# Orders of their own for the last four attention rounds, the last three query tiles' exponentials transposed by TensorE

## The chip, the cores and the metric

The kernel runs on one core of a Trainium2 chip. The metric is the device time of one execution in microseconds. Of the kernel before three executions were timed; their median is the time it is known by. One more execution was taken with the hardware profiler, and all rows in this document come from that one. TensorE is the matmul engine (PE in the rows), VectorE is DVE, ScalarE is ACT, GpSimd is POOL, and SP issues the DMAs.

## What is computed

One transformer-like layer over 1024 latent tokens of width 1024 and 256 context tokens. Its parts: layer norm and modulation, one input projection, latent attention with 8 heads, a Fourier mixing branch, gates, one output projection, and a residual with a last layer norm. What matters here, cut from the reference:

```python
s = einsum("bqhd,bkhd->bhqk", q, k) / sqrt(96)        # 1280 keys: 256 context, 1024 latent
p = softmax(s, axis=-1)
attn = einsum("bhqk,bkhv->bqhv", p, v)
y = concatenate([attn * silu(g_mla), four * silu(g_f)], -1) @ w_out + b_out
x_new = layer_norm(2 ** 0.25 * x + gate * y, post_ln_g, post_ln_b)
```

## The kernel before

Products that need f32 accuracy are done as three matmuls on a high and a low part (`mm3`); softmax weights and V are split into two f16 parts.

Attention works in 32 rounds, one for each pair of query tiles of one head: `Pair` n has head n // 4 and the query tiles j = 0 and 1, each 128 queries by 1280 keys. The steps for a tile:

- S: the scores, on TensorE, into PSUM. `SL[j]` holds 1024 latent keys, and `SC`, which both tiles share, the context keys.
- m, c, t: minima over both parts, with a copy into the SBUF tile `E`, and the bias, on VectorE.
- x: the exponential of 1280 columns in place, on ScalarE.
- h, l: the f16 high part on ScalarE and the low part by subtraction on GpSimd, into a tile `EH`, and then one transposing DMA from `EH` to half of `ET` (line 1058). There are three buffers each of `E`, `EH` and `ET`.
- P0, P1: PV over five key blocks each, on TensorE, for both tiles of a pair at a time, into a PSUM tile of the pool `tr`, which has three buffers.
- Ra, Rv: the two parts of PV are added into `ats` by ScalarE and VectorE.

The loop at the end of the attention runs n from 0 to 33. Round n does S of pair n + 1, the exponentials of pairs n and n + 1, and PV of pair n - 2 (`LAG`). The order inside a round is a list of names, written out by hand: `SEQ`, and `SEQ2` from round 30 on. A mark ' means pair n in place of n + 1. For the five engines the order of issue is this one (`manual_schedule`); work from behind the loop may be put between by the tile scheduler, which fixes one order for each engine when the kernel is built.

The output projection sums 8 blocks of 128 rows (kt), in the order 4, 5, 6, 7 (Fourier branch) and 0, 1, 2, 3 (attention). Each needs its block of w_out loaded (`load_wo`) and split, and its block of the mixed activations split (`prep`: one step for w_out, one for the mix, each a copy on ScalarE and a subtraction on VectorE, called by `s`). `INSIDE` lists for each kt the round of its load and the round in which its steps are put into the list of steps. `E` in the order lists is an early projection step: one kt of row tile 0 or 1, six matmuls of 512 columns into `SL[0]` or `SL[1]`, used from round 31 on. Row tile 3 uses `SC` and a `tr` buffer, row tile 2 two `tr` buffers.

`gate_rows` issues two DMAs that fetch the gate of the residual, as one of the `fills` (round `FT['g']`, 29). After the last round `sum_rows`, `finish_rows` and `finish_pair` divide by the sums: a reciprocal on VectorE, broadcasts on GpSimd, four transposes on TensorE for each half, and products on VectorE and GpSimd. Then come kt 2 and 3 and `finish`, the residual and layer norm of each row tile (128 rows).

The code for transposing on TensorE stands in the kernel, and `ON_PE` is empty: `T` (`e_tr`) transposes some key blocks of `E` in f32 into a `tr` tile, in the cuts a, b, c of 4, 4 and 2 blocks (`KCUT`), and `U` (`e_out`) writes high and low part from there into `ET`, with ScalarE and VectorE.

Of the kernel before, what the change touches and what calls it, by code (L numbers as in the profile page):

```python
# [25 lines left out]
HEADS = 8  # L26
# [5 lines left out]
PVT = '1' == '1'  # L32
RP = '0' == '1'
MAN = 'PVAGS'
ON_PE = set()
KCUT = ((0, 1, 2, 3), (4, 5, 6, 7), (8, 9))
SEQ = "h0' s S0b f ga S0a P0 S1a P1 S1c S0c m0 l0' gv S1b c0 x1' h1' t0 Ra m1 Rv x0 c1 t1 l1' f ga gv".split()
PVL = eval('[[0,1,2,3,4],[5,6,7,8,9]]')
TABP = eval('(("to", 0),)')
HI_CUTS = (((0, 1280, 'a'),), ((0, 1280, 'a'),))  # L40
LO_CUTS = (((0, 1280, 'p'),), ((0, 1280, 'p'),))
RBE = 'p'
GME = 'p'
SEQ2 = "h0' S0b f ga S0a E P0 S1a P1 S1c S0c m0 l0' gv S1b c0 x1' h1' t0 Ra m1 Rv x0 c1 t1 l1' f ga gv s s E s s E s s E".split()
NSEQ2 = int('30')
NLAST = int('28')
HI_LAST = HI_CUTS
LO_LAST = LO_CUTS


INSIDE = ((4, 18, 20, True), (5, 28, 31, False), (6, 29, 31, False), (7, 30, 31, False), (0, 31, 32, False), (1, 32, 32, False))
NHI = int('8')
EB = int('3')
FT = eval("{'k': [0, 0, 1], 'q': [1, 2], 'r': 4, 'p': [5, 5], 'v': [11, 14, 15, 16, 17], 'g': 29}")
ETB = int('3')
LAG = int('2')
EHB = int('3')
# [8 lines left out]
def tile_hybrid_block(ctx: ExitStack, tc: tile.TileContext, a, out, dbg=None):  # L66
# [926 lines left out]
    class Pair:  # L993
# [47 lines left out]
        def hi(self, j):  # L1041

            self.EH[j] = pools["e"].tile([P, 2, 1280], F16, tag="EH", name="EH", bufs=EHB)
            for c0, c1, eng in (HI_LAST if self.n >= NLAST else HI_CUTS)[j]:
                o, i = self.EH[j][:, 0, c0:c1], self.E[j][:, c0:c1]
                if eng == "a":
                    nc.scalar.activation(out=o, in_=i, func=AF.Copy)  # L1047
                else:
                    {"v": nc.vector, "p": nc.gpsimd}[eng].tensor_scalar(out=o, in0=i, scalar1=1.0, scalar2=0.0,
                                                                        op0=ALU.mult, op1=ALU.add)  # L1050

        def lo(self, j):
            for c0, c1, eng in (LO_LAST if self.n >= NLAST else LO_CUTS)[j]:
                cs = slice(c0, c1)
                {"v": nc.vector, "p": nc.gpsimd}[eng].tensor_tensor(  # L1055
                    out=self.EH[j][:, 1, cs], in0=self.E[j][:, cs], in1=self.EH[j][:, 0, cs], op=ALU.subtract)
            self.weights_t()
            nc.sync.dma_start(out=self.ET[:, j], in_=self.EH[j].rearrange("p l k -> p (l k)"), transpose=True)
# [63 lines left out]
    def sum_rows(h):  # L1122

        rinv[h] = small.tile([P, 8], F32, tag="ri", name="ri", bufs=3)
        nc.vector.reciprocal(out=rinv[h], in_=sums[h])

    def finish_rows(pair, half):

        rb = small.tile([P, 4, 2, 64], F32, tag="h", name="rb", bufs=4)
        for e in range(2):  # L1130
            o, i = rb[:, :, e, :], rinv[2 * pair + e][:, 4 * half:4 * half + 4].unsqueeze(2).to_broadcast([P, 4, 64])
            if RBE == "a":
                nc.scalar.activation(out=o, in_=i, func=AF.Copy)
            else:
                nc.gpsimd.tensor_scalar(out=o, in0=i, scalar1=1.0, scalar2=0.0, op0=ALU.mult, op1=ALU.add)
        rbs[pair, half] = rb

    def finish_pair(pair, half):
        hs = slice(512 * half, 512 * half + 512)
        rb = rbs[pair, half]  # L1140
        pt = tr(f"r{pair}{half}")
        for i in range(4):
            nc.tensor.transpose(pt[:, i * P:(i + 1) * P], rb[:, i].rearrange("p a b -> p (a b)"), ident)

        def out():
# [59 lines left out]
    NP = 4 * HEADS  # L1205
    fills = {n: [] for n in range(NP + LAG)}
    fills[0] = [lambda: build_qt(0, 1, False)] + [lambda i2=i2: build_v(0, i2, False) for i2 in range(3, 5)]
    for h in range(HEADS - 1):
        if h % 2:
            for c in range(3):  # L1210
                fills[4 * h + FT['k'][c]].append(lambda c=c, p=(h + 1) // 2: build_kt(p, c, BP))
        for hf in range(2):
            fills[4 * h + FT['q'][hf]].append(lambda hf=hf, h1=h + 1: build_qt(h1, hf, BQ))
        if h % 2:
            p = h // 2
# [66 lines left out]
    with tc.manual_schedule(engines={{'P': ET.PE, 'V': ET.DVE, 'A': ET.Activation, 'G': ET.Pool, 'S': ET.SP}[c] for c in MAN}):  # L1282
        for n in range(NP + LAG):
            nxt, prv = pairs.get(n + 1), pairs.get(n - LAG)
            h = n // 4
            if nxt is not None and (n + 1) % 4 == 0:
                start_head((n + 1) // 4)
            fill = fills[n]
            for kt, r, _, _ in INSIDE:
                if n == r:  # L1290
                    load_wo(kt)
            for kt, _, r, beside in INSIDE:
                if n == r:
                    steps += prep(kt, 2, how=split_p) if beside else prep(kt)
            for op in (SEQ2 if n >= NSEQ2 else SEQ):
                k = int(op[1]) if len(op) > 1 and op[1].isdigit() else 0
                who, c = nxt, op[0]
                if op[-1] == "'":
                    who = pairs.get(n)
                if c in "PR":  # L1300
                    who = prv
                if c in "SmctxhlPRTU" and who is None:
                    continue
                if c in "hlTU" and who.on_pe(k) != (c in "TU"):
                    continue
                if c == "S":
                    for hf in range(3):
                        if len(op) == 2 or op[2] == "abc"[hf]:
                            who.s_lat(k, hf)
                elif c == "m":  # L1310
                    who.max_lat(k)
                elif c == "c":
                    who.max_ctx(k)
                elif c == "t":
                    who.bias(k)
                elif c == "x":
                    who.exp(k)
                elif op == "ga" or op == "gv":
                    for ab in ("a" if op == "ga" else "av"):
                        for f in late[ab]:  # L1320
                            f()
                        late[ab].clear()
                elif c == "T":
                    who.e_tr(k, "abc".index(op[2]))
                elif c == "U":
                    who.e_out(k, "abc".index(op[2]))
                elif c == "h":
                    who.hi(k)
                elif c == "l":
                    who.lo(k)  # L1330
                elif c == "P":
                    lst = PVL[int(op[1])]
                    who.pv(lst, first=lst[0] == 0, last=lst[-1] == 9)
                elif c == "R":
                    who.pv_out() if op == "Rv" else who.pv_top()
                elif c == "f":
                    if fill:
                        late["on"] = n > 0
                        fill.pop(0)()
                        late["on"] = False  # L1340
                elif c == "s":
                    if steps:
                        steps.pop(0)()
                elif c == "E":
                    if n >= NP - 1 and early:
                        t, i = early.pop(0)
                        done.add((t, i))
                        if t not in pss:
                            pss[t] = po_t(t)
                        out_mms(pss[t], t, i)  # L1350
            while fill:
                fill.pop(0)()
            for ab in "av":
# [164 lines left out]
```

## Time and profile before

| | us |
|---|---|
| median of three executions | 620.54 (619.78 to 621.72) |
| the profiled execution | 624.29 |
| its span | 622.3 |
| TensorE busy in it | 581.2 |
| VectorE busy | 381.6 |
| ScalarE busy | 311.2 |
| GpSimd busy | 283.2 |

The busy share is an average over stages with different limits: input projection, attention (its last PV ends at 533.46 us), output projection. For this change the last 140 us count. A row of a timeline gives start, duration, engine, line, operation, and in brackets the idle time of the engine before it with what ended that time; rows of one kind are merged (xN). A row of the windows gives for one stretch the busy time of each engine, the granted clock of TensorE as a share of 2.4 GHz, and the DMA traffic.

### The profile page before, as it was taken

The numbers are of one execution on the slowest core, as the hardware profiler recorded it, in microseconds if no ns is written. First come the engines' busy times: TensorE is split into PE (matmuls) and PEld (weight loads), VectorE is DVE, ScalarE is ACT, GpSimd is POOL, SyncE is SP. The second block draws the span as 40 slices with busy tenths as digits, with TensorE's granted clock in tenths as the row PEclk, the third lists the DMA queues.
The fourth block names the chain that finished last, engine by engine and source line by source line (L and its number), as shares of the span: only waits on it lengthen the run. The fifth ranks groups of instructions, "written<-read, shape, count | busy, mean of one in ns | idle before, by whom it ended". The sixth has DMA issues, their size and how long they took to land.

```text
span 622.3 us, 9537 instructions
## 1 busy us (share of the span) xinstructions
PE 581.2 (93%) x3491; PEld 463.1 (74%) x3491; DVE 381.6 (61%) x871; ACT 311.2 (50%) x478; POOL 283.2 (46%) x221
## 2 busy tenths in 40 slices
PE   7999999999999998999899899999989878999992
PEld 6877777888899998998665677666657545788882
DVE  5448317811005597787676767676756626669897
ACT  2322621211024344468898799888978755310000
POOL 2123315011012258357777877888989762310000
PEclk9899999999999999999998999999989988999997
DMA  9999029000001041214999999999999999610332
GB/s 287 312 313 378 20 68 313 15 1 0 1 0 52 1 140 35 68 43 85 195 182 185 172 185 184 176 202 200 173 177 194 219 228 201 253 76 0 137 135 102
DMA packets 199703, 88.81 MB, mean 143 GB/s; under 512 B 168205, under 2 KB 189965, under 8 KB 199657
## 3 DMA queue, kind: packets, MB, share of 16 engines
q1 hardware_dynamic: 199656, 88.21, 61.2%
q8 instruction: 27, 0.44, 0.3%
q14 instruction: 20, 0.16, 0.1%
HBM read 41.39 MB, written 4.20 MB: 73 GB/s over the span
## 4 chain that ended last, share of the span: by engine, by line
PE 61%; DMA 14%; ACT 8%; DVE 7%; issue 5%; POOL 3%; SPq 1%; DVEq 0%; POOLq 0%; ACTq 0%
PE g L323 11%; DMA ET<-EH 11%; PE SL L1194 7%; PE fin L323 7%; PE o L1194 5%; ACT EH L1047 3%; POOL EH L1055 3%; ACT E L1038 3%; PE pv L1097 2%; DMA wada<-in_w_ada_dram 2%; PE tm L138 2%; PE tm L139 2%; PE tm L140 2%; PE pv L1100 2%; PE SL L138 2%
## 5 line engine op out<-in xcount | busy, mean ns | idle before, releaser
L1055 POOL TENSOR_TENSOR EH<-E,EH 128x1280 f16<-128x1280 f32 x64 | 168.3, 2634 | 48.9 <-ACT EH L1047 47.8
L1047 ACT ACTIVATE EH<-E 128x1280 f16<-128x1280 f32 x64 | 81.2, 1269 | 27.3 <-DMA ET<-EH 26.0
L1019 DVE TENSOR_SCALAR_CACHE_REDUCE E<-SL 128x1024 f32<-128x1024 f32 x64 | 78.1, 1221 | 19.9 <-POOL EH L1055 17.4
L1038 ACT ACTIVATE E<-E,mx 128x1280 f32<-128x1280 f32 x64 | 86.8, 1357 | 5.1 <-DVE mx L1032 4.6
L323 PE MATMUL fin<-h,wh 128*128 128x512 f32 x192 | 65.3, 408 | 0.0
L323 PE MATMUL g<-h,wh 128*128 128x512 f32 x192 | 60.3, 394 | 1.0 <-DVE upm L385 1.0
L1097 PE MATMUL pv<-ET,V 128*128 128x256 f16 x320 | 48.1, 283 | 12.4 <-DMA ET<-EH 8.4
L138 PE MATMUL SL<-KTh,QT 96*128 96x512 f32 x128 | 55.5, 433 | 0.5 <-DVE tf L972 0.5
L1097 PEld LDWEIGHTS <-V 128*128 128x128 f16 x320 | 27.5, 101 | 35.3 <-issue 31.3
L140 PE MATMUL SL<-KTh,QT 96*128 96x512 f32 x128 | 50.9, 398 | 0.0
L139 PE MATMUL SL<-KTl,QT 96*128 96x512 f32 x128 | 50.9, 397 | 0.0
L1019 DVE TENSOR_SCALAR_CACHE_REDUCE E<-SC 128x256 f32<-128x256 f32 x64 | 26.8, 419 | 32.9 <-PE SC L140 32.4
L323 PEld LDWEIGHTS fin<-h,wh 128*128 128x128 f32 x192 | 36.3, 190 | 10.3 <-issue 2.9
L323 PEld LDWEIGHTS g<-h,wh 128*128 128x128 f32 x192 | 36.0, 188 | 9.8 <-issue 1.4
L354 POOL TENSOR_SCALAR h<-xnT,mod 128x512 f32<-128x512 f32 x15 | 12.9, 859 | 63.4 <-ACT xnT L340 27.6
L323 PE MATMUL g<-h,wl 128*128 128x512 f32 x96 | 37.8, 394 | 0.0
L323 PE MATMUL fin<-h,wl 128*128 128x512 f32 x96 | 37.1, 395 | 0.0
L432 ACT ACTIVATE gt<-g,cols 128x512 f32<-128x512 f32 x12 | 8.1, 689 | 56.1 <-PE g L323 56.1
L1100 PE MATMUL pv<-ET,V 128*64 128x256 f16 x320 | 34.3, 291 | 0.0
L114 ACT ACTIVATE rs_t<-mvf,eps 128x1 f32<-128x1 f32 x8 | 2.4, 295 | 62.0 <-DVE mvf L1405 42.3
L1415 POOL TENSOR_TENSOR xr<-xr,lng 128x256 f32<-128x256 f32 x2 | 1.4, 723 | 67.2 <-ACT xr L1414 67.2
L355 DVE TENSOR_TENSOR h<-h,h 128x512 fp32r<-128x512 f32 x15 | 13.6, 907 | 30.0 <-POOL h L354 22.7
(343 smaller groups left out, 1430.4 us busy)
## 6 DMA issues: line engine op xcount, KB each, us to landing
wada<-in_w_ada_dram SPq DMA_DIRECT2D x32, 256.0 KB, 5.8
x<-in_x_dram SPq DMA_DIRECT2D x8, 512.0 KB
wgate<-in_w_ada_dram SPq DMA_DIRECT2D x8, 512.0 KB, 6.7
wor<-in_w_out_dram SPq DMA_DIRECT2D x8, 512.0 KB, 4.4
xr<-in_x_dram SPq DMA_DIRECT2D x8, 512.0 KB, 6.3
out_dram<-xr SPq DMA_DIRECT2D x15, 256.0 KB, 3.4
wr<-in_w_in_dram SPq DMA_DIRECT2D x6, 512.0 KB, 5.4
wtr<-in_w_in_dram SPq DMA_DIRECT2D x4, 416.0 KB, 6.2
```

What stands on the lines that cost most here:

```text
L138: nc.tensor.matmul(ps, lhsT=sh, rhs=mh, start=(start and i == 0), stop=False)
L139: nc.tensor.matmul(ps, lhsT=sh, rhs=ml, start=False, stop=False)
L140: nc.tensor.matmul(ps, lhsT=sl, rhs=mh, start=False, stop=(i == n - 1))
L323: nc.tensor.matmul(ps, lhsT=(w.hi, w.lo, w.hi)[p][k][:, cs], rhs=h[:, p // 2], start=(k == 0 and p == 0), stop=(k == 7 and p == 2))
L355: nc.vector.tensor_tensor(out=hh[:, 1], in0=h, in1=hh[:, 0].bitcast(F32), op=ALU.subtract)
L1019: nc.vector.tensor_scalar(out=dst, in0=src, scalar1=0.0, scalar2=3e38, op0=ALU.add, op1=ALU.min, accum_out=self.mx[:, c:c + 1])
L1038: nc.scalar.activation(out=self.E[j], in_=self.E[j], func=AF.Exp, scale=-1.0, bias=self.mx[:, j:j + 1], accum_out=sums[self.h][:, qt:qt + 1])
L1047: nc.scalar.activation(out=o, in_=i, func=AF.Copy)
L1055: {"v": nc.vector, "p": nc.gpsimd}[eng].tensor_tensor(out=self.EH[j][:, 1, cs], in0=self.E[j][:, cs], in1=self.EH[j][:, 0, cs], op=ALU.sub ...
L1097: nc.tensor.matmul(po, lhsT=v.rearrange("p l c -> p (l c)"), rhs=e, start=(kt == 0), stop=False)
L1100: nc.tensor.matmul(po[64 * g:64 * g + 64], lhsT=v[:, 0], rhs=e, start=False, stop=(kt >= 8), tile_position=(0, 64 * g))
L1194: nc.tensor.matmul(ps[c], lhsT=st, rhs=w[:, c[0]:c[1]], start=(i == 0 and st is mh and w is wh), stop=(i == 7 and st is ml))
```

## The change

Rounds 30 to 33 get an order list each (`LAST`). Tile 1 of pair 30 and both tiles of pair 31 are put into `ON_PE`: their `h` and `l` and their DMA are skipped, and `T` and `U` stand in the lists instead. Loads and splits move: kt 5 is loaded in round 29 (28 before), kt 6 in 30 (29), kt 1 in 31 (32); the splits of kt 0 and 1 come in round 33 (31 and 32), and the gate rows in round 33 (29). Sums and their broadcasts for the last head pair are done by `r` at the end of round 31, and `finish_pair` stands ahead of the remaining steps. Early projection steps are spread otherwise. `HI_LAST` and `LO_LAST` were equal to `HI_CUTS` and `LO_CUTS`, so that edit changes nothing.

```diff
-ON_PE = set()
+ON_PE = {(30, 1), (31, 0), (31, 1)}
...
-SEQ2 = "h0' S0b f ga S0a E P0 S1a P1 S1c S0c m0 l0' gv S1b c0 x1' h1' t0 Ra m1 Rv x0 c1 t1 l1' f ga gv s s E s s E s s E".split()
-NSEQ2 = int('30')
...
-INSIDE = ((4, 18, 20, True), (5, 28, 31, False), (6, 29, 31, False), (7, 30, 31, False), (0, 31, 32, False), (1, 32, 32, False))
+LAST = {30: "h0' S0b S0a P0 S1a P1 S1c S0c m0 l0' S1b c0 x1' T1a' T1b' t0 U1a' T1c' Ra m1 Rv x0 c1 t1 U1b' U1c'".split(),
+        31: "x1' E T0a' T0b' P0 U0a' T0c' P1 U0b' U0c' Ra Rv s T1a' T1b' U1a' E T1c' U1b' U1c' s r".split(),
+        32: "E E s s P0 P1 Ra Rv E E s s".split(),
+        33: "E P0 P1 Ra Rv E".split()}
...
+INSIDE = ((4, 18, 20, True), (5, 29, 31, False), (6, 30, 31, False), (7, 30, 31, False), (0, 31, 33, False), (1, 31, 33, False))
...
-FT = eval("{'k': [0, 0, 1], 'q': [1, 2], 'r': 4, 'p': [5, 5], 'v': [11, 14, 15, 16, 17], 'g': 29}")
+FT = eval("{'k': [0, 0, 1], 'q': [1, 2], 'r': 4, 'p': [5, 5], 'v': [11, 14, 15, 16, 17], 'g': 33}")
...
-            for op in (SEQ2 if n >= NSEQ2 else SEQ):
+            for op in LAST.get(n, SEQ):
...
+                elif c == "r":
+                    sum_rows(HEADS - 1)
+                    for hf in range(2):
+                        finish_rows(HEADS // 2 - 1, hf)
...
             if n == NP + LAG - 1:
+                for hf in range(2):
+                    finish_pair(HEADS // 2 - 1, hf)
                 while steps:
                     steps.pop(0)()
-            if n == NP + LAG - 1:
-                sum_rows(HEADS - 1)
-                for hf in range(2):
-                    finish_rows(HEADS // 2 - 1, hf)
-                    finish_pair(HEADS // 2 - 1, hf)
```

## Rows read from the trace of the kernel before

**Rows 1.** Windows: us; busy us (instructions) of each engine; PEclk; DMA share; GB/s

```profile
505.00:510.00 5.00, 1.53 (x4) 0.91 (x5) 1.07 (x4) 4.08 (x5) 2.62 (x1) 0.75 1.05 211
...
580.00:608.00 28.00, 28.00 (x137) 23.38 (x136) 24.82 (x52) 0.89 (x3) 0.00 (x0) 1.00 0.41 144
```

**Rows 2.** Timeline of TensorE: start us, us, engine, line, operation, idle before

```profile
353.71 0.64 PE L830 MATMUL qh<-ident,q_sb 128*96 128x128 f32 x4 [1.67 <-DVE at L1116]
...
498.25 0.71 PE L1097 MATMUL pv<-ET,V 128*128 128x256 f16 x5 [1.88 <-ACT E L1038]
...
502.75 0.63 PE L1194 MATMUL SL<-woh,mh 128*128 128x512 f32 x2
...
508.47 0.79 PE L1194 MATMUL SC<-woh,mh 128*128 128x512 f32 x1 [4.16 <-DVE E L1019]
...
517.63 1.15 PE L1194 MATMUL SL<-woh,mh 128*128 128x512 f32 x2 [1.89 <-ACT mh L103]
...
524.78 0.72 PE L1097 MATMUL pv<-ET,V 128*128 128x256 f16 x5
525.43 0.52 PE L1100 MATMUL pv<-ET,V 128*64 128x256 f16 x5
525.88 0.72 PE L1097 MATMUL pv<-ET,V 128*128 128x256 f16 x5
...
533.46 0.73 PE L1194 MATMUL SL<-woh,mh 128*128 128x512 f32 x2
```

**Rows 3.** The chain that ended last, in order of time: start us, us, what

```profile
498.05 7.71 DMA ET<-EH
...
545.48 0.44 PE r L1143 x4
...
565.98 22.18 PE SL L1194 x96
```

**Rows 4.** Timeline of the SP queue, rounds 28 and 29

```profile
488.43 0.58 SPq L1166 DMA_DIRECT2D wor<-in_w_out_dram  x1
489.17 3.94 SPq L1058 DMA_TRANSPOSE ET<-EH  x1
493.16 3.19 SPq L1058 DMA_TRANSPOSE ET<-EH  x1
...
498.05 5.72 SPq L1058 DMA_TRANSPOSE ET<-EH  x1
```

**Rows 5.** Timeline of ScalarE: the f16 copies of tiles (30,1) and (31,1)

```profile
505.84 1.27 ACT L1047 ACTIVATE EH<-E 128x1280 f16<-128x1280 f32 x1 [4.99 <-DMA ET<-EH]
...
513.88 1.27 ACT L1047 ACTIVATE EH<-E 128x1280 f16<-128x1280 f32 x1 [2.24 <-DMA ET<-EH]
```

**Rows 6.** Groups by line and shape, 330 to 520 us: count | busy us, mean ns | idle

```profile
L1019 DVE TENSOR_SCALAR_CACHE_REDUCE E<-SL 128x1024 f32<-128x1024 f32 x49 | 59.8, 1221 | 15.2 <-POOL EH L1055 13.1 <-PE SL L140 0.4
...
L1116 DVE TENSOR_TENSOR at<-pv,pvt 64x256 f32<-64x256 f32 x26 | 10.9, 420 | 13.8 <-ACT pvt L1106 13.6
...
L1143 PE MATMUL r<-ident,rb 128*128 128x128 f32 x24 | 3.6, 272 | 0.0
L777 DVE TENSOR_TENSOR V<-v,V 128x512 f16<-128x512 f32 x5 | 3.4, 684 | 0.3 <-ACT V L775 0.3
L103 ACT ACTIVATE woh<-wor 128x1024 fp32r<-128x1024 f32 x3 | 3.1, 1047 | 0.0
...
L775 ACT ACTIVATE V<-v 128x512 f16<-128x512 f32 x5 | 2.9, 586 | 0.5 <-PE v L140 0.5
```

**Rows 7.** Windows behind the TensorE gaps that ended at 353.71 and 517.63

```profile
353.70:357.20 3.50, 3.47 (x23) 2.29 (x24) 3.30 (x8) 3.50 (x6) 3.50 (x3) 1.00 0.88 170
...
517.70:521.10 3.40, 3.40 (x8) 2.17 (x9) 3.40 (x3) 3.40 (x4) 1.55 (x2) 0.51 1.13 281
```

**Rows 8.** Timeline of VectorE behind the last PV

```profile
545.96 0.74 DVE L1146 SCALAR_TENSOR_TENSOR gt<-r,vscale,gt 128x512 f32<-128x512 f32 x1
...
551.15 1.21 DVE L104 TENSOR_TENSOR ml<-gt,mh 128x1024 fp32r<-128x1024 f32 x1
...
557.95 2.48 DVE L1401 TENSOR_TENSOR y<-SL,gate 128x512 f32<-128x512 f32 x4 [5.59 <-PE SL L1194]
```

More of the change, by code (lines that the diff above doesn't have):

```diff
@@ L43 @@
 GME = 'p'
-SEQ2 = "h0' S0b f ga S0a E P0 S1a P1 S1c S0c m0 l0' gv S1b c0 x1' h1' t0 Ra m1 Rv x0 c1 t1 l1' f ga gv s s E s s E s s E".split()
-NSEQ2 = int('30')
-NLAST = int('28')
-HI_LAST = HI_CUTS
-LO_LAST = LO_CUTS
-INSIDE = ((4, 18, 20, True), (5, 28, 31, False), (6, 29, 31, False), (7, 30, 31, False), (0, 31, 32, False), (1, 32, 32, False))
+LAST = {30: "h0' S0b S0a P0 S1a P1 S1c S0c m0 l0' S1b c0 x1' T1a' T1b' t0 U1a' T1c' Ra m1 Rv x0 c1 t1 U1b' U1c'".split(),
[3 more added lines that the diff above has]
+INSIDE = ((4, 18, 20, True), (5, 29, 31, False), (6, 30, 31, False), (7, 30, 31, False), (0, 31, 33, False), (1, 31, 33, False))
 NHI = int('8')
 EB = int('3')
-FT = eval("{'k': [0, 0, 1], 'q': [1, 2], 'r': 4, 'p': [5, 5], 'v': [11, 14, 15, 16, 17], 'g': 29}")
+FT = eval("{'k': [0, 0, 1], 'q': [1, 2], 'r': 4, 'p': [5, 5], 'v': [11, 14, 15, 16, 17], 'g': 33}")
 ETB = int('3')
@@ L1043, in hi @@
             self.EH[j] = pools["e"].tile([P, 2, 1280], F16, tag="EH", name="EH", bufs=EHB)
-            for c0, c1, eng in (HI_LAST if self.n >= NLAST else HI_CUTS)[j]:
+            for c0, c1, eng in HI_CUTS[j]:
                 o, i = self.EH[j][:, 0, c0:c1], self.E[j][:, c0:c1]
@@ L1052, in lo @@
         def lo(self, j):
-            for c0, c1, eng in (LO_LAST if self.n >= NLAST else LO_CUTS)[j]:
+            for c0, c1, eng in LO_CUTS[j]:
                 cs = slice(c0, c1)
```

## The prediction

> **What bounds the kernel now.** I read the busy time by stretch first [rows 1]. From 580 to 608 us TensorE is busy for the whole 28 us at a granted clock of 1.00; from 505 to 510 it is busy for 1.53 of 5 us, at 0.75 (1.00 is 2.4 GHz, 0.50 is 1.2 GHz). So whatever the last attention rounds lose is lost for good: behind them stands only output projection that fills TensorE to its end.
>
> TensorE in order of time shows the losses [rows 2]. It stands for 1.88 us before 498.25 (the PV of round 30, pair 28), 4.16 us before 508.47 and 1.89 us before 517.63: 7.9 us. Work at 1.2 GHz comes on top. A 512-column matmul goes at 0.231 us each at the higher clock (96 in 22.18 us [rows 3]); one half of a PV (P0 or P1) takes 1.1 us (524.78 to 525.88 [rows 2]). From 508.47 to 515.74, where the third gap begins, TensorE did 9 such matmuls and two PV halves, 4.3 us of work in 7.3 us; from 517.63 to 524.78 it did 23, 5.3 us in 7.15. That is 4.8 us more, 12.7 us in all.
>
> The SP queue tells why [rows 4]. An undisturbed transposing DMA holds SP for 3.19 us, (28,0) with a w_out load ahead 3.94, and (29,0), behind a w_out load and the two gate rows, 5.72; that one needs 7.71 us to land [rows 3]. Since only three EH buffers exist, ScalarE's f16 copies of (30,1) and (31,1) stand 4.99 and 2.24 us until an older transfer lands [rows 5], and with them exponentials, PV and the w_out splits.
>
> **The change part by part.** *Removed.* Of the last four DMA transposes three go, (30,1), (31,0) and (31,1), with their 1.27 us copies on ScalarE [rows 5] and their subtractions on GpSimd; only (30,0) still takes an EH buffer, that of (28,1), so the waits of 4.99 and 2.24 us go.
>
> *Loads moved.* The load of kt 5 no longer stands ahead of (28,0), nor kt 6 and the gate ahead of (29,0). (28,0) then starts at 488.43 in place of 489.17, (28,1) follows after 3.2 us at 491.6 (493.16 before), and lands 5.1 us later (493.16 to the PV at 498.25 is 5.1 [rows 2, 4]), at 496.8. So the PV of pair 28 starts 1.5 us earlier. The load of kt 5 now stands ahead of (29,0), which starts at about 495.5, (29,1) at 499.6; that one lands near 504.8, and its PV is due after 507. Loads of kt 6 and 7 precede (30,0), which by the slowest row (7.71) lands by 512; its PV is due after 517. Loads of kt 0 and 1 and the gate rows have no transpose behind them. All are hidden; if a slot for a load came free late, only the tail's loads queue behind it, and they are wanted after 540.
>
> *Added on TensorE.* 3 tiles of 10 f32 blocks. Four such transposes move the chain on by 0.44 us [rows 3]: 30 cost 3.3 us, all on the path.
>
> *Added on ScalarE and VectorE.* Per tile two evictions of 512 columns and one of 256, an f16 copy and a subtraction each. The V build does the same on the same shapes: 0.59 us and 0.68 us [rows 6]. ScalarE has room; on VectorE and PSUM they make new waits:
>
> - Round 30. S of (31,1) ends near 501.3 (4.5 us behind the PV, as before from 498.25 to 502.75 [rows 2]). Transposes a and b take to 502.2. Transpose c takes the third PSUM buffer, which pair 28's PV holds until Rv. VectorE gives: eviction a (copy to 502.4, subtraction to 503.1), the minimum over 1024 columns (1.22 us [rows 6]) to 504.3, Rv (0.42 [rows 6]) to 504.7. TensorE waits 502.2 to 504.75: 2.55 us, with the first projection step (E) and round 31 queued behind.
> - Round 31. E (1.4), a and b of (31,0) (0.9), PV (1.1), c (0.2) and PV (1.1) bring TensorE to 509.7. ScalarE's chain is then Ra (0.4, like Rv), the w_out copy of kt 5 (1.05 [rows 6]), evictions a, b, c (0.6, 0.6, 0.4, c by its 256 columns) and the mix copy (1.05): 514.1 with TensorE's c between. TensorE waits 0.45 us for Rv and, after its transposes and a second E, from 512.75 to 514.15 for kt 5: 1.4 us. Its low part costs 0.25 more.
> - Rounds 32 and 33. The splits of kt 6 and 7 run beside E and PV: 0.15 us.
>
> With 0.4 us left before pair 28's PV (496.4 to 496.8), new idle is 5.2 us; less 0.7 if the scheduler drops the three projection matmuls on SC, which it hoisted to 508.47 before, into the 1.4 us hole.
>
> *The clock.* The gap of 1.89 us was followed by a stretch of 3.4 us at 0.51, one of 1.67 us before 353.71 by none [rows 2, 7]. One such stretch does half its work, a loss of 1.7 us. The bounds for the holes of 2.55 and 1.4 us are no stretch and two, 0 and 3.4 us. I take one, 1.7: 2.55 lies above both gaps, 1.4 below both.
>
> *Moved at the end.* Reciprocal and broadcast of the row sums leave the end of round 33 for round 31, where they cost VectorE 0.2 us and GpSimd, idle by then, nothing that is waited for; the last pair's scaling goes ahead of the splits of kt 0 and 1, two VectorE operations of 0.74 us [rows 8]. TensorE has the four ready kt's of row tiles 2 and 3 meanwhile: 48 matmuls, 11 us; without that cover the price is 1.5 us. The low part of kt 3 was issued at 551.15, and VectorE started on results at 557.95 [rows 8]; with the sums done early, it can only come sooner. Behind that the tail moves as a block.
>
> *The sum.* Lost before 12.7; lost after 3.3 + 5.2 - 0.7 + 1.7 = 9.5. Gain 3.2 us. A second way: before, after the last PV at 533.46, 328 of 384 matmuls were left; after, the last E ends at 527.45 with 336 left, 8 x 0.231 = 1.85 us more, so 6.0 - 1.85 = 4.2 without clock loss and filler, 3.2 with them. The profiled execution took 624.29 us against a median of 620.54 (0.994): 621.1 becomes 617.3.
>
> **A rule against the change.** The profile gives each f32 transpose a duration of 272 ns, but four follow within 0.44 us [rows 3, 6]. The Trainium skill, "TensorE: Matmul & The Clock Gate", Part 4: PE-mode transpose, gives 275 ns for one in a kernel's context; by 30 such in a row the sum would be 8.3 us instead of 3.3, an estimate that would turn the gain into a loss of 1.8 us. The duration agrees, the spacing here is shorter, and the measurement decides.
>
> **The rivals.** *The clock stays down (slower).* Between 505 and 512.75 TensorE has 7.3 us of work, 2.2 of it transposes, in pieces. If the clock stays at 1.2 GHz from the first hole until kt 5 is in, that stretch ends 6.7 us later (doubled it is 7.3 us, of which ScalarE's fixed chain covers 0.6), and one more fall behind it costs 1.7: 4.2 + 0.7 - 8.4, a loss of 3.5 us, 624.0. It decides once the clock costs more than 4.9 us. The same section of the skill says that the higher clock does not engage for transposes, which speaks for it. Against it: before, even behind a hole of 4.16 us the slow work cost 3.0 us, and matmuls stand between the transposes. In the trace of before transposes never stand alone.
>
> *The holes close.* The static scheduler puts projection matmuls into them and the clock holds: gain up to 12.7 - 3.3 = 9.4, 611.2; midway to the forecast is 614. For it speaks that it hoisted one before; against it that in the first hole SL[1] and SC are still taken.
>
> *The gain goes back.* Two low stretches, or a hoisted matmul or tail operation that blocks a queue (the SC matmuls hoisted to 508.47 stood ahead of a PV [rows 2]): gain 0 to 1.9, 618.7 to 622.4. VectorE is 24.8 of 28 us busy in the last stretch [rows 1], so a bunched tail ends there too.
>
> **How the numbers follow.** Forecast 0.45; holes close 0.25; gain goes back 0.22; clock stays down 0.08. Within 0.3%, 1.9 us, is about what a measurement of this kernel cannot tell from no change. Faster 0.45 + 0.25 = 0.70, same 0.22, slower 0.08. The range goes from 612.0 (most of the holes closed) to 622.0, leaving out the best end and the slower case.
>
> **What would show it.** Right: the PV of pair 28 near 497; no f16 copy behind that of (30,0); transposes four in 0.44 us; a hole of 2 to 3 us ahead of transpose c of (30,1), ended by VectorE; a hole ahead of kt 5's projection, ended by ScalarE; at most one low stretch; the last PV near 525 and an unbroken TensorE behind. Wrong: the clock at 0.5 through round 31, evictions far over 0.59 and 0.68 us, or TensorE idle after 528.

## The result and the profile after

The changed kernel takes 613.78 us (612.83 to 614.80, four executions) against 620.27 (619.78 to 621.72) beside it: ratio 0.989, interval 0.9869 to 0.991, a gain of 6.5 us (5.6 to 8.1). Forecast were 617.3 and a gain of 3.2: right in sign, inside the range, half in size. Measured twice more (e8, e17) the ratio is 0.987 and 0.9889.

The profiled execution took 614.02 us with a span of 612.2. First TensorE's timeline through the transposing rounds, as [rows 2] of before: start, duration, engine, line, operation, idle before.

```profile
492.59 0.40 PE L137 MATMUL SL<-KTh,QT 96*128 96x512 f32 x1
...
494.38 0.71 PE L1096 MATMUL pv<-ET,V 128*128 128x256 f16 x5 [0.24 <-ACT E L1037]
...
498.88 1.04 PE L1073 MATMUL et<-ident,E 128*128 128x128 f32 x8
500.89 0.44 PE L1073 MATMUL et<-ident,E 128*128 128x128 f32 x2 [0.97 <-DVE ET L1083]
...
505.96 0.44 PE L1073 MATMUL et<-ident,E 128*128 128x128 f32 x2 [0.51 <-DVE ET L1083]
...
507.32 1.09 PE L1073 MATMUL et<-ident,E 128*128 128x128 f32 x8
508.17 0.71 PE L1193 MATMUL SL<-woh,mh 128*128 128x512 f32 x2
...
511.45 0.72 PE L1193 MATMUL SL<-woh,mh 128*128 128x512 f32 x2 [1.42 <-ACT mh L102]
...
524.55 0.52 PE L1099 MATMUL pv<-ET,V 128*64 128x256 f16 x5
524.99 0.72 PE L1193 MATMUL SL<-woh,mh 128*128 128x512 f32 x2
```

The gaps of 1.88, 4.16 and 1.89 us are gone; 0.24, 0.97, 0.51 and 1.42 stand there now. Eight transposes move TensorE on by 0.85 us (507.32 to 508.17). The windows of the same kernel (us; busy us and instructions of PE, PEld, DVE, ACT, POOL; PEclk; DMA share; GB/s), the first as in [rows 1]:

```profile
505.00:510.00 5.00, 4.49 (x34) 3.25 (x33) 3.22 (x5) 3.46 (x7) 0.00 (x0) 1.00 0.95 261
...
492.60:525.00 32.40, 29.26 (x183) 20.70 (x181) 19.45 (x36) 18.36 (x29) 8.62 (x6) 1.00 0.78 182
...
525.00:547.40 22.40, 22.40 (x102) 18.36 (x102) 20.61 (x16) 9.47 (x10) 6.91 (x3) 1.00 0.59 211
...
547.40:612.20 64.80, 55.29 (x263) 45.88 (x262) 58.38 (x127) 3.16 (x10) 1.41 (x2) 0.95 0.26 90
```

TensorE works for 4.49 of the 5 us in which it worked for 1.53, and its clock is 1.00 throughout. The third row matters more: from the last PV to VectorE's first product of the residual (y, line 1401), VectorE is busy for 20.61 of 22.40 us. In the kernel before the same stretch looked like this:

```profile
533.50:557.90 24.40, 24.40 (x111) 19.96 (x111) 13.76 (x13) 5.79 (x6) 8.80 (x6) 1.00 0.52 194
```

There VectorE stood for 10.6 of 24.4 us while TensorE never stopped. VectorE's timeline behind the last PV after the change, as [rows 8]:

```profile
527.12 1.41 DVE L1145 SCALAR_TENSOR_TENSOR gt<-r,vscale,gt 128x512 f32<-128x512 f32 x2 [1.18 <-PE r L1142]
528.44 1.89 DVE L103 TENSOR_TENSOR wol<-wor,woh 128x1024 fp32r<-128x1024 f32 x1
530.26 2.33 DVE L103 TENSOR_TENSOR ml<-gt,mh 128x1024 fp32r<-128x1024 f32 x1
532.51 4.56 DVE L103 TENSOR_TENSOR wol<-wor,woh 128x1024 fp32r<-128x1024 f32 x2
537.00 2.35 DVE L103 TENSOR_TENSOR ml<-gt,mh 128x1024 fp32r<-128x1024 f32 x2
539.27 1.21 DVE L103 TENSOR_TENSOR wol<-wor,woh 128x1024 fp32r<-128x1024 f32 x1
540.41 1.21 DVE L103 TENSOR_TENSOR ml<-gt,mh 128x1024 fp32r<-128x1024 f32 x1
541.54 5.75 DVE L1396 SCALAR_TENSOR_TENSOR xr<-xr,bo 128x1024 f32<-128x1024 f32 x5
547.44 1.29 DVE L1401 TENSOR_TENSOR y<-SL,gate 128x512 f32<-128x512 f32 x2
```

From 527.12 up to y VectorE has no gap of more than 0.15 us, and the wait of 5.59 us ahead of y [rows 8] is gone. From y on (the last row of the windows) it is busy for 58.38 of 64.80 us.

To compare kernels I measure from one point, S: the first matmul of the scores of (31,0), S0b in the list of round 30 (the row at 492.59 above; 494.82 in the trace before). What lies ahead of S differs between executions of the same kernel by up to 4.5 us (S at 494.82 in the profile of before, at 490.37 in e1), so no gain is read from it. All in us, from one profiled execution each; three of the change itself (after, e8, e17) differ by 0.9 from S to the end. Timed is the median, with that of the kernel before beside it.

| kernel | S to last PV | last PV to y | S to TensorE's end | S to the end | timed (before) |
|---|---|---|---|---|---|
| before | 38.6 | 24.5 | 115.7 | 127.5 | |
| e1, before again | 39.4 | 24.5 | 116.5 | 128.2 | 622.72 (622.02) |
| e2, loads alone | 36.6 | 27.2 | 117.2 | 127.5 | 620.30 (622.02) |
| e10, sums alone | 39.6 | 20.5 | 116.4 | 125.1 | 618.17 (622.80) |
| e3, change with DMA transposes | 35.7 | 22.4 | 113.4 | 122.2 | 615.41 (622.02) |
| after | 32.4 | 22.4 | 110.1 | 119.6 | 613.78 (620.27) |
| e8, the change again | 32.5 | 22.4 | 110.2 | 119.6 | 614.97 (622.81) |
| e17, the change again | 33.2 | 22.4 | 110.9 | 120.5 | 614.12 (621.98) |
| e4, change, loads put back | 35.2 | 22.4 | 112.8 | 122.7 | 616.70 (622.02) |
| e6, change, sums late | 32.4 | 33.8 | 119.6 | 130.1 | 625.94 (622.81) |
| e12, change, more VectorE work | 32.5 | 22.4 | 110.2 | 124.6 | 618.49 (622.80) |
| e14, change, GpSimd's products on VectorE | 32.4 | 27.3 | 110.2 | 123.9 | 618.61 (621.98) |
| e18, change, row by row | 33.6 | 22.2 | 111.2 | 120.5 | 614.32 (621.07) |
| e7, holes closed | 30.7 | 22.5 | 108.5 | 118.1 | 612.47 (622.81) |

So the pair of profiles differs by 10.1 us: 2.2 ahead of S, which can't be put down to the change, 6.2 up to the last PV, 2.0 from there to y, less 0.4 behind y.

### The profile page after: what moved, and what is told of

Its sections match the earlier page's. It is cut to its first block, busy times and chain, and to the rows that moved or that the text cites. A ratio compares the mean times of both kernels' runs of the same rounds, so it can differ in the third digit from the quotient of the medians.

```text
span 612.2 us, 9594 instructions
## 1 busy us (share of the span) xinstructions
PE 577.5 (94%) x3521; PEld 462.7 (76%) x3521; DVE 388.5 (63%) x880; ACT 311.4 (51%) x484; POOL 275.4 (45%) x218
## 4 chain that ended last, share of the span: by engine, by line
PE 51%; DMA 15%; ACT 8%; DVE 7%; SPq 7%; POOL 6%; issue 5%; DVEq 0%; POOLq 0%; ACTq 0%
DMA ET<-EH 13%; PE g L322 11%; PE SL L1193 7%; PE o L1193 5%; PE fin L322 5%; POOL EH L1054 4%; ACT EH L1046 3%; SPq L245 3%; SPq L218 3%; ACT E L1037 2%; PE tm L137 2%; PE tm L138 2%; PE tm L139 2%; PE pv L1096 2%; PE pv L1099 1%
## 5 line engine op out<-in xcount | busy, mean ns | idle before, releaser
L1054 POOL TENSOR_TENSOR EH<-E,EH 128x1280 f16<-128x1280 f32 x61 | 160.4, 2634 | 39.2 <-ACT EH L1046 38.0
L1046 ACT ACTIVATE EH<-E 128x1280 f16<-128x1280 f32 x61 | 77.4, 1269 | 19.7 <-DMA ET<-EH 18.6
L1096 PE MATMUL pv<-ET,V 128*128 128x256 f16 x320 | 45.8, 274 | 13.3 <-DMA ET<-EH 10.3
L1099 PE MATMUL pv<-ET,V 128*64 128x256 f16 x320 | 33.0, 282 | 0.0
```

The costliest lines, as they stand in the source:

```text
L1054: {"v": nc.vector, "p": nc.gpsimd}[eng].tensor_tensor(out=self.EH[j][:, 1, cs], in0=self.E[j][:, cs], in1=self.EH[j][:, 0, cs], op=ALU.sub ...
L1096: nc.tensor.matmul(po, lhsT=v.rearrange("p l c -> p (l c)"), rhs=e, start=(kt == 0), stop=False)
L1099: nc.tensor.matmul(po[64 * g:64 * g + 64], lhsT=v[:, 0], rhs=e, start=False, stop=(kt >= 8), tile_position=(0, 64 * g))
```

## The experiments

### The parts one by one: e1, e2, e4, e10

e1 is the kernel before, unchanged. e2 gives it the changed loads alone, e4 takes them out of the change, e10 gives the kernel before the early sums alone.

```diff
--- e2, against the kernel before (and 'g': 33 in FT)
-INSIDE = ((4, 18, 20, True), (5, 28, 31, False), (6, 29, 31, False), (7, 30, 31, False), (0, 31, 32, False), (1, 32, 32, False))
+INSIDE = ((4, 18, 20, True), (5, 29, 31, False), (6, 30, 31, False), (7, 30, 31, False), (0, 31, 32, False), (1, 31, 32, False))
--- e4, against the change (and 'g': 29 in FT)
-INSIDE = ((4, 18, 20, True), (5, 29, 31, False), (6, 30, 31, False), (7, 30, 31, False), (0, 31, 33, False), (1, 31, 33, False))
+INSIDE = ((4, 18, 20, True), (5, 28, 31, False), (6, 29, 31, False), (7, 30, 31, False), (0, 31, 33, False), (1, 32, 33, False))
--- e10, against the kernel before
-            for op in (SEQ2 if n >= NSEQ2 else SEQ):
+            for op in (SEQ2 if n >= NSEQ2 else SEQ) + ["r"] * (n == NP - 1):
...
+                elif c == "r":
+                    sum_rows(HEADS - 1)
+                    for hf in range(2):
+                        finish_rows(HEADS // 2 - 1, hf)
...
-                sum_rows(HEADS - 1)
                 for hf in range(2):
-                    finish_rows(HEADS // 2 - 1, hf)
                     finish_pair(HEADS // 2 - 1, hf)
```

> The kernel before, unchanged, profiled again. Theory 'clock': the profiled execution of before was 3.8 us over its median because TensorE's clock fell four times between 300 and 525 us; another profile shows fewer low stretches, and its time is nearer to 620.3 by about 1.7 us for each one fewer. Rival 'profiler': the profiled execution of before is always about 3.8 us longer than the others, with the same four low stretches. Ratio 1.000 by both.

> Before, with only the loads of kt 5, 6, 1 and the gate rows moved as in the change (rounds 29, 30, 31, 33); splits and orders stay, all transposes stay with the DMA. Theory 'TensorE account': the PV of pair 28 comes 1.5 us earlier, the waits of the f16 copies of (30,1) and (31,1) shrink but stay: gain 1 to 2.5 us. Rival 'SP queue': relief of the queue is most of what the change brought: gain 4 us or more.

> The change with its loads of kt 5, 6, 1 and the gate rows put back to rounds 28, 29, 32 and 29. Theory 'TensorE account': the PV of pair 28 comes 1.5 us later again, the later transfers keep their slack: 1 to 2 us slower than the change, a gain of 4.5 to 5.5 us against before. Rival 'SP queue': 4 us or more slower than the change.

> Before, with only the last head pair's reciprocal and broadcasts moved from the end of round 33 to the end of round 31. Theory 'first result': in ten profiles the end lies 63.7 to 65.0 us behind VectorE's first product of the tail; with the sums early, kt 3 is ready sooner and the first product comes about 22.5 us behind the last PV in place of 24.5: gain about 2 us, TensorE's own end later against the last by less. Rival 'TensorE account': no hole of TensorE is touched between 525 and 607, within 0.7 us of before.

e1: ratio 1.001 (0.9982 to 1.0038). Its profiled execution took 620.38 us, so profiling alone does not make the 624.29 of the first profile. The clock theory fits in the main: there the granted clock was 0.50 from 333.4 to 336.8 and from 456.3 to 459.7 us, in e1 it was 1.00 from 20 us up to S; S comes 4.5 us earlier, where two such stretches at 1.7 us make 3.4.

e2: 0.9971 (0.995 to 0.9992), 1.7 us. Its last PV comes 2.1 to 2.9 us earlier, but 2.7 are lost again between it and y, where TensorE waits 1.86 us for GpSimd's broadcast of the sums. e4: 616.70, 0.9907 (0.9874 to 0.994), so the change keeps 5.3 of its gain without the loads; 2.21 us of idle time stand ahead of pair 28's PV again.

e10: 0.992 (0.9889 to 0.9952), 4.6 us, for a step that the forecast priced at nothing. Its profile is the cleanest comparison of all, as it reached S at the same time as e1 (490.42 and 490.37). VectorE in e1, then in e10:

```profile
547.65 1.22 DVE L104 TENSOR_TENSOR ml<-gt,mh 128x1024 fp32r<-128x1024 f32 x1
554.29 1.89 DVE L1401 TENSOR_TENSOR y<-SL,gate 128x512 f32<-128x512 f32 x3 [5.42 <-PE SL L1194]
```

```profile
539.68 1.21 DVE L104 TENSOR_TENSOR ml<-gt,mh 128x1024 fp32r<-128x1024 f32 x1
540.82 6.14 DVE L1398 SCALAR_TENSOR_TENSOR xr<-xr,bo 128x1024 f32<-128x1024 f32 x5
550.45 1.29 DVE L1403 TENSOR_TENSOR y<-SL,gate 128x512 f32<-128x512 f32 x2 [3.49 <-PE SL L1194]
```

The last matmul of TensorE in e1, then in e10:

```profile
606.55 0.28 PE L1194 MATMUL SL<-woh,ml 128*128 128x256 f32 x1
```

```profile
606.58 0.28 PE L1194 MATMUL SL<-woh,ml 128*128 128x256 f32 x1
```

TensorE ends at the same moment, y comes 3.84 us earlier, and the span is 3.1 us shorter (618.6 to 615.5). TensorE's end does not set the time. In both y still waits for TensorE, which is busy without a break from the last PV on; it comes earlier because fewer matmuls of the other row tiles stand ahead of it. The window of e10 from the last PV to y has 94 instructions of TensorE, where the kernel before has 111:

```profile
530.00:550.40 20.40, 20.40 (x94) 16.82 (x94) 16.31 (x12) 5.80 (x6) 6.90 (x3) 1.00 0.63 232
```

### Without the early sums: e6

The change, with `r` taken out of the list of round 31 and sums, broadcasts and `finish_pair` behind the remaining steps of round 33.

```diff
-        31: "x1' E T0a' T0b' P0 U0a' T0c' P1 U0b' U0c' Ra Rv s T1a' T1b' U1a' E T1c' U1b' U1c' s r".split(),
+        31: "x1' E T0a' T0b' P0 U0a' T0c' P1 U0b' U0c' Ra Rv s T1a' T1b' U1a' E T1c' U1b' U1c' s".split(),
...
-                for hf in range(2):
-                    finish_pair(HEADS // 2 - 1, hf)
                 while steps:
                     steps.pop(0)()
+                sum_rows(HEADS - 1)
+                for hf in range(2):
+                    finish_rows(HEADS // 2 - 1, hf)
+                    finish_pair(HEADS // 2 - 1, hf)
```

> The change with the last head pair's sums, broadcasts and scaling put back behind all splits at the end of round 33. Theory 'tail order': the scaled rows of kt 3 come late, row tiles 0 to 2 end later, VectorE is bunched at the end: the stretch from TensorE's last matmul to the end goes from 9.5 back to 11 us or more, and the time is 1.5 to 3 us above the change. Rival 'block': the tail moves as a block whatever the order: within 0.7 us of the change.

625.94 us, 1.004 (1.0016 to 1.0065), against 614.97 of the change timed beside it (e8): 11.0 us, where 1.5 to 3 were expected. Up to the last PV nothing differs (32.4 us). Behind it TensorE waits 5.21 us for GpSimd's broadcast, and y comes late:

```profile
547.15 1.12 PE L1142 MATMUL r<-ident,rb 128*128 128x128 f32 x4 [5.21 <-POOL rb L1134]
```

```profile
560.76 1.29 DVE L1403 TENSOR_TENSOR y<-SL,gate 128x512 f32<-128x512 f32 x2 [8.00 <-PE SL L1193]
```

In this kernel the early sums and `finish_pair` ahead of the splits, which e6 takes back together, are worth more than the whole change. Here TensorE ends 9.5 us later too, so e6 alone does not tell the two engines apart; e10 does.

### The transposes: e3, e9, e5, e8

e3 and e9 are one kernel: the change with `ON_PE` empty and the DMA transposes back in the new lists. e5 issues each transpose into `et` twice. e8 is the change, beside e9.

```diff
--- e3, e9
-ON_PE = {(30, 1), (31, 0), (31, 1)}
+ON_PE = set()
...
+LAST = {30: "h0' S0b S0a P0 S1a P1 S1c S0c m0 l0' S1b c0 x1' h1' t0 Ra m1 Rv x0 c1 t1 l1'".split(),
+        31: "h0' x1' E P0 l0' P1 h1' Ra Rv l1' s E s r".split(),
--- e5
-                nc.tensor.transpose(pt[:, i * P:(i + 1) * P], self.E[j][:, kt * P:(kt + 1) * P], ident)
+                for _ in range(2):
+                    nc.tensor.transpose(pt[:, i * P:(i + 1) * P], self.E[j][:, kt * P:(kt + 1) * P], ident)
```

> The change without its transposes on TensorE: loads, splits, early projection steps and sums where the change has them, but all tiles copied, subtracted and transposed by DMA. Theory 'TensorE account': the f16 copies of (30,1) and (31,1) wait for EH again and TensorE has holes of over 5 us in rounds 30 to 32; it saves 3.5 us of transposes: against before a gain of 0 to 2.5 us. Rival 'orders': the orders alone bring most of it, gain 4 us or more.

> The change itself once more, beside the others of this call. Theory 'holes': its time is 1.5 to 3 us below the same orders with all transposes left to the DMA (e9). Rival 'orders alone': the two are within 0.7 us.

> The same kernel as e3: the orders, loads and sums of the change, all tiles transposed by DMA. Theory 'holes': TensorE stands for 3 us and 4 us in rounds 31 and 32 and loses 1.7 us or more to the clock, against 3.5 us of transposes saved: 1.5 to 3 us slower than the change of this call. Rival 'orders alone': within 0.7 us of it.

> The change with each of its 30 transposes issued twice into the same PSUM block. Theory 'price': 30 more cost up to 3.3 us on TensorE ahead of the last PV, the holes hide about 1, so the last PV, VectorE's first result and the end all come 2 to 3.3 us later. Rival 'hidden': the evictions set the pace, less than 1 us.

e3: 615.41, 0.9891 (0.9868 to 0.9914): 6.6 us without one transpose on TensorE, so the rival "orders" held and the theory (0 to 2.5) did not. Timed once more, e9 took 617.77, 0.9906 (0.9873 to 0.9938), and beside it e8 614.97, 0.987 (0.9845 to 0.9895): 2.8 us for the transposes, with intervals that overlap. By the profiles it is 1.7 to 2.7: from S to the end e3 took 122.2 and e9 122.3, the change 119.6, 119.6 (e8) and 120.5 (e17). With the DMA the waits of [rows 5] stay, and the granted clock is 0.90 from S to the last PV of e3 (1.00 in the change); ScalarE and TensorE of e3:

```profile
500.12 1.27 ACT L1046 ACTIVATE EH<-E 128x1280 f16<-128x1280 f32 x1 [4.37 <-DMA ET<-EH]
...
508.37 1.27 ACT L1046 ACTIVATE EH<-E 128x1280 f16<-128x1280 f32 x1 [2.46 <-DMA ET<-EH]
```

```profile
502.27 1.23 PE L1096 MATMUL pv<-ET,V 128*128 128x256 f16 x5 [3.06 <-DMA ET<-EH]
...
512.12 1.22 PE L1193 MATMUL SL<-woh,mh 128*128 128x512 f32 x2 [4.05 <-ACT mh L102]
```

e5 took 614.75, 0.9855 (0.982 to 0.9889): the timing doesn't show 30 more transposes. Its profile is 2.1 us longer from S to the end than the change's (1.2 longer than that of e17): 30 more at 0.11 us are 3.3 us of TensorE work, and the holes of 0.97 and 0.51 shrink to 0.54 and 0.

### The holes closed: e7, e16

The change, with a projection step between transposes b and c of (30,1), the PV of pair 29 ahead of c of (31,0), and kt 5 split in round 30, its mix first.

```diff
+LAST = {30: "h0' S0b S0a P0 S1a P1 S1c S0c m0 l0' S1b c0 x1' s T1a' T1b' t0 U1a' E T1c' Ra m1 Rv x0 c1 t1 U1b' U1c'".split(),
+        31: "x1' T0a' T0b' P0 U0a' P1 T0c' U0b' U0c' Ra Rv s T1a' T1b' U1a' E T1c' U1b' U1c' s r".split(),
...
+INSIDE = ((4, 18, 20, True), (5, 29, 30, False), (6, 30, 31, False), (7, 30, 31, False), (0, 31, 33, False), (1, 31, 33, False))
...
+                    steps += prep(kt, 2, how=split_p) if beside else prep(kt)[::-1] if kt == 5 else prep(kt)
...
+                    if n >= NP - 2 and early:
```

> The change with its three holes closed: the first projection step goes ahead of transpose c of (30,1) in round 30, transpose c of (31,0) behind the second PV half, and the split of kt 5's mix from round 31 to round 30, ahead of its w_out split. Theory 'TensorE account': holes of 0.97, 0.51 and 1.42 us go, 2 to 2.9 us faster than the change, about 611. Rival 'next wait': ScalarE or VectorE, which get a mix split (1.05 and 1.2 us) in round 30, open another hole, or VectorE at the end is the bound: less than 1 us faster.

> The kernel with the holes closed again, for comparison in the same call: 612.5 us, 2 to 3 under the change; end 118.1 us behind the start of the scores of (31,0).

612.47 us, 0.983 (0.9803 to 0.9857), and 612.02, 0.9851 (0.9821 to 0.988): 2.5 and 2.1 us under the change timed beside them, the best kernel of this study. TensorE of e7:

```profile
501.88 0.63 PE L1073 MATMUL et<-ident,E 128*128 128x128 f32 x4 [1.05 <-ACT ET L1081]
...
507.15 0.65 PE L1073 MATMUL et<-ident,E 128*128 128x128 f32 x4 [0.50 <-DVE ET L1083]
```

The hole of 1.42 is gone; one of 1.05 is left, ended by an eviction of ScalarE.

### What bounds the tail: e11, e12, e14, e15, e17, e18, e19

e12 does the product y twice for the first half of each row tile. e11 takes the row tiles' products with ALPHA from VectorE to GpSimd. e14 (e15 on the kernel with the holes closed) takes GpSimd's two last products `gt` and that of b_out and the gate to VectorE. e18 writes the remaining matmuls of row tiles 0 to 2 row by row; e19 is e15 with that order. e17 is the change beside e14.

```diff
--- e12
+            for _ in range(2 if j == 0 else 1):
+                nc.vector.tensor_tensor(out=y, in0=ps[c], in1=gate[0][:, cs], op=ALU.mult)
--- e11
-        nc.vector.scalar_tensor_tensor(out=xr, in0=xr, scalar=ALPHA, in1=bo, op0=ALU.mult, op1=ALU.add)
+        nc.gpsimd.tensor_scalar(out=xr, in0=xr, scalar1=ALPHA, scalar2=0.0, op0=ALU.mult, op1=ALU.add)
+        nc.gpsimd.tensor_tensor(out=xr, in0=xr, in1=bo, op=ALU.add)
--- e14, and e15 on e7
-            {'v': nc.vector, 'p': nc.gpsimd}[GME].tensor_tensor(
+            {'v': nc.vector, 'p': nc.gpsimd}['v' if pair == 3 else GME].tensor_tensor(
...
-    nc.gpsimd.tensor_tensor(out=bo, in0=bo, in1=gate[0], op=ALU.mult)
+    nc.vector.tensor_tensor(out=bo, in0=bo, in1=gate[0], op=ALU.mult)
--- e18, and e19 on e15
-    for i in range(8):
-        for t in range(3):
+    for t in range(3):
+        for i in range(8):
             if (t, i) not in done:
                 out_mms(pss[t], t, i)
-    for t in range(3):
         finish(t, pss[t])
```

> The change with one product of the tail (y, 128x512 from PSUM, about 0.6 us) done twice in each of the 8 row tiles, 4.8 us more of VectorE work. Theory 'VectorE bounds the tail': with 2.3 us of idle time left in its last 64.7 us, 2.5 to 4.8 us slower than the change, all of it behind the first product. Rival 'TensorE bounds the tail': less than 1 us slower.

> The change with the first step of the residual (x times a constant plus the bias row, 1.22 us for each of 8 row tiles on VectorE) done by GpSimd, which is idle there, in two operations. Theory 'VectorE bounds the tail': 9.8 us of VectorE's last 64.7 go, the stretch from its first product to the end shrinks by 3 us or more until TensorE's end sets it, and so does the time. Rival 'TensorE bounds the tail': within 1 us of the change.

> The change, with the last pair's product gt and the product of b_out and the gate moved from GpSimd to VectorE. In the change, four of VectorE's splits of 1024 columns run beside these three GpSimd operations and take 8.56 us from start to start, where undisturbed ones follow at 1.14 us, 4.6 us for four. Theory (VectorE bounds everything behind the last PV, and GpSimd's work stretches it): VectorE gets 2 x 0.6 + 1.14 = 2.4 us of work and loses 4.0 us of stretch, so the end comes 1.6 us earlier against the start of the scores of (31,0), 118.0 in place of 119.6, and the time is 1.6 us under that of the change. Rival (TensorE's end sets the time): no difference. Second rival (the added work counts, the stretch does not): 2.4 us later.

> The kernel with the holes closed (first projection step in round 30, kt 5 split before the transposes), with the same two products on VectorE. Theory: 1.6 us under the kernel with the holes closed, about 611; end 116.5 us behind the start of the scores of (31,0) in place of 118.1. Rival (TensorE's end sets the time): as the kernel with the holes closed.

> The change again, for comparison in the same call: ratio 0.987 to the kernel before, end 119.6 us behind the start of the scores of (31,0).

> The change, with the remaining projection matmuls of row tiles 0 to 2 written row tile by row tile in place of block by block, so that the scheduler puts 16 fewer matmuls of the other rows ahead of row tile 0's last one (16 x 0.231 = 3.7 us). Theory A (the end comes 64 to 65 us behind VectorE's first product, and that product waits only for TensorE's order): first product 3.7 us earlier, time 3.7 us under the change. Theory B (in the change VectorE is busy without a break from the last PV on, so its work in all sets the end): first product earlier where work can be put behind it, but the end within 1 us of the change.

> The kernel with the holes closed and the two products on VectorE, which waited 6.5 us for TensorE ahead of its first product, with the same order by row tiles. Theory A and B both expect a gain over the run without that order, by up to the 6.5 us of idle time: some 611 us. Theory B expects it 1.6 us under the kernel with the holes closed as well, since GpSimd no longer stretches VectorE's splits; if it stays above that kernel, the products on VectorE cost more than the stretch.

e12: 618.49 us, 0.9914 (0.9884 to 0.9943). It does 8 more products of 0.6 us, 4.8 in all; TensorE ends 110.2 us behind S as in the change, and the end comes 5.0 us later (124.6). So what VectorE does behind y sets the end here.

e11: 622.89, 0.9995 (0.9971 to 1.0018): it was to relieve VectorE and stretched it instead. VectorE, then GpSimd, of e11:

```profile
581.21 7.81 DVE L1422 SCALAR_TENSOR_TENSOR xr<-xr,rsf,lnb 128x512 f32<-128x512 f32 x4
```

```profile
581.15 2.40 POOL L1397 TENSOR_TENSOR xr<-xr,bo 128x1024 f32<-128x1024 f32 x1
583.52 1.49 POOL L1396 TENSOR_SCALAR xr<-xr 128x1024 f32<-128x1024 f32 x1
585.10 2.71 POOL L1397 TENSOR_TENSOR xr<-xr,bo 128x1024 f32<-128x1024 f32 x1
```

The change does these four in 2.69 us. GpSimd stretches the splits ahead of y as well, and y comes 27.1 us behind the last PV in place of 22.4. So e11 could not tell what less work on VectorE brings.

e14: 618.61, 0.9943 (0.9922 to 0.9964), 4.5 us above the change timed beside it (e17, 614.12, 0.9889 with 0.9857 to 0.9922). None of its theories had that. VectorE of e14:

```profile
536.19 2.35 DVE L103 TENSOR_TENSOR wol<-wor,woh 128x1024 fp32r<-128x1024 f32 x2
538.46 2.35 DVE L103 TENSOR_TENSOR ml<-gt,mh 128x1024 fp32r<-128x1024 f32 x2
540.73 5.76 DVE L1396 SCALAR_TENSOR_TENSOR xr<-xr,bo 128x1024 f32<-128x1024 f32 x5
553.05 1.29 DVE L1401 TENSOR_TENSOR y<-SL,gate 128x512 f32<-128x512 f32 x2 [6.57 <-PE SL L1193]
```

The splits are no longer stretched, and VectorE is through at 546.5, 20.8 us behind the last PV against 22.3 in the change: the 1.6 us that the theory expected, nearly. Then it waits 6.57 us. The scheduler has put more matmuls of row tiles 2 and 3 ahead of row tile 0's last one, 65 in place of 43 from the last PV to y: 27.3 us of TensorE work lie there, where the change has 22.4. TensorE is never idle and ends where it did (110.2); the end is 4.3 us later. e15 shows the same on the closed kernel: 616.47, 0.9909 (0.9869 to 0.9949), a wait of 6.53 us.

e18 put 16 matmuls fewer ahead of row tile 0's last one, and brought nothing: 614.32, 0.9875 (0.9821 to 0.9929). Row tile 0's last matmuls (`ml`) in the change, then in e18:

```profile
546.78 0.61 PE L1193 MATMUL SL<-woh,ml 128*128 128x512 f32 x2
```

```profile
543.22 1.08 PE L1193 MATMUL SL<-woh,ml 128*128 128x512 f32 x4
```

That is 21.8 and 18.1 us behind the last PV, 3.7 us earlier in e18, but y comes at 22.4 and 22.2: VectorE had no gap ahead of y in the change, so theory B held. In e19, where it had one, the order took the wait from 6.53 to 2.89 us and the way from S to the end from 123.1 to 119.8; the kernel with the holes closed has 118.0 (e16). e19 took 615.29, 0.989 (0.9828 to 0.9953), where both theories had some 611.

Together: the end comes when VectorE is through, and y comes at the later of two times, VectorE's own work behind the last PV and TensorE's place for row tile 0's last block. In the kernel before the second was late; in the change both fall together (547.29 and 547.40 us).

## Why the prediction was right in sign and half in size

**The step that failed** is "with the sums done early, it can only come sooner. Behind that the tail moves as a block." The account was kept to TensorE's end, and the moved sums stood in it at nothing, since 48 matmuls covered them. TensorE was covered; VectorE was not. It stood for 10.6 us behind the last PV, and from y to the end it is 63.7 to 65.3 us in all runs but e11 and e12, so the end follows y and not TensorE. e10 puts the term at 3.1 us by the profiles (S to the end against e1; 2.4 against the first profile of before) and 4.6 by the times; e14 shows that cover on TensorE is itself the delay. [Rows 1], busy share 28.00 against 24.82, hid this: a full TensorE says what is late only if its last matmul is what the end waits for, and [rows 8] already showed VectorE waiting 5.59 us for row tile 0.

This is about half of what was missing. The other half lies in two terms of TensorE's account that were too large, the clock and the holes.

**The clock** was charged with 1.7 us and cost nothing: 1.00 from 492.6 to 525, against 0.75 in the one stretch of [rows 1]. The rival in which it stays down did not come about. As the hole of 2.55 us was not there either, how the clock would have answered to it is open.

**The holes** were charged with 5.2 less 0.7 and measured 3.14. Ahead of transpose c of (30,1) 0.97 stands for 2.55: it took the buffer of transpose a, free after a's own subtraction, not that of the PV, and so did not wait for minimum and Rv. ScalarE, then VectorE, after the change:

```profile
499.52 0.60 ACT L1081 ACTIVATE ET<-et 128x512 f16<-128x512 f32 x1 [2.54 <-PE et L1073]
```

```profile
500.15 0.69 DVE L1083 TENSOR_TENSOR ET<-et,ET 128x512 f16<-128x512 f32 x1 [1.09 <-ACT ET L1081]
500.76 1.22 DVE L1018 TENSOR_SCALAR_CACHE_REDUCE E<-SL 128x1024 f32<-128x1024 f32 x1
...
502.01 0.43 DVE L1115 TENSOR_TENSOR at<-pv,pvt 64x256 f32<-64x256 f32 x1
```

Behind round 31's E the forecast of 1.4 met 1.42. The 0.45 for Rv, 0.25 for kt 5's low part and 0.15 of the later splits were nothing; 0.51 ahead of c of (31,0) was not foreseen.

**The 8 matmuls left over** (1.85 us in the second way) came to 3: 331 stand behind the last PV and 328 did before, and from there to TensorE's end it is 77.70 us, against 77.03. The scheduler hoisted 11 projection matmuls on SC ahead of the last PV, 2.5 us that the forecast had left behind it; so the last PV comes 32.4 us behind S, 527.2 on the clock of the profile before, where 525 was forecast.

**The balance from S**: TensorE's end gained 5.6 us (115.7 to 110.1) where 3.2 were forecast: 1.7 of clock and 1.4 of holes not lost, less 0.7. Of this 0.7 the transposes make 0.3, as all 30 took 3.6 us by the starts of their rows where 3.3 were forecast; the rest was not traced. Behind TensorE's end another 2.3 us went (11.8 to 9.5), which stood in no term. The sum, 7.9, answers to the 7.8 and 7.9 us of e8 and e17.

**What was right**: the PV of pair 28 starts 1.79 us behind S, forecast 1.98 (496.8 to 494.82); transposes four in 0.44 us, evictions 0.60 and 0.69 us; no f16 copy behind that of (30,0); TensorE unbroken behind the last PV. Thirty transposes were forecast to cost 3.3 us, and doubling them cost 2.1 in the profile. The Trainium skill, "TensorE: Matmul & The Clock Gate", Part 4: PE-mode transpose, gives 275 ns for one, which would make 8.3 us of thirty in a row, an estimate; the traces don't agree, as eight move on in 0.85 us.

**What was luck**: the rival "the holes close" named the right time (614), but of its reasons only the clock that holds came true; the hole ahead of c of (30,1) shrank by a buffer that was free early, and not by matmuls put into it, and the tail was in none of its terms. That the time lies inside the range owes as much to its lower end, which was set for closed holes.

## What to carry to other kernels

An engine that is busy to its end need not be what the end waits for: look at which engine has work left behind it, when that engine got its first input, and what stood in the order ahead of that input. "Covered" holds for one engine only; write beside each cover who waits behind the covering work. When a static scheduler fills the cover, a change elsewhere can reorder it, so compare the wait ahead of the first result, not the busy share.

## What the runs showed of the hardware

Beside GpSimd's products VectorE's operations took longer. In the change the four splits from 528.44 to 537.00 take 8.56 us from start to start, while GpSimd works from 527.95 to 534.87; undisturbed ones follow at 1.14 us (539.27 to 540.41), 4.6 for four. In e14, without GpSimd, they take 1.22 each. GpSimd after the change:

```profile
527.95 3.56 POOL L1147 TENSOR_TENSOR gt<-at,gt 128x512 f32<-128x512 f32 x2 [11.85 <-DVE gt L1145]
531.47 3.40 POOL L1386 TENSOR_TENSOR bo<-bo,gate 128x1024 f32<-128x1024 f32 x1
```

The Trainium skill, "SBUF — State Buffer", Who interferes with whom, says that a VectorE instruction with two SBUF inputs contends with a GpSimd instruction that reads SBUF; the splits and the stretched operation of e11 have two such inputs, and the traces agree.

The length of a TensorE gap alone doesn't tell whether the clock falls. Behind the 1.86 us ahead of a PV at 493.78 in e1 it fell; behind 2.21 us ahead of the same PV in e4 it did not. Window of e1, then of e4:

```profile
494.40:497.80 3.40, 3.40 (x14) 1.82 (x13) 1.23 (x2) 1.97 (x3) 3.08 (x2) 0.50 1.62 288
```

```profile
498.00:501.40 3.40, 3.39 (x26) 2.19 (x27) 1.23 (x2) 2.58 (x3) 2.93 (x2) 1.00 1.19 279
```

Transposes between matmuls did not bring it down: 1.00 in the change's rounds (492.6 to 525 us), and 1.00 with 60 of them in e5 (491.5 to 526).
